# A hybrid decoder layer on one core: the output projection cut into two passes, one head group started later, and the low halves of a stretch of weights given to one engine

## The chip, the cores and the metric

The kernel runs on one core of one Trainium2 chip. The metric is the device time of one execution in microseconds, the median of several executions; lower is better. The engines are TensorE (PE in the rows; PEld its weight loads), VectorE (DVE), ScalarE (ACT), GpSimd (POOL), and SyncE (SP), which here only issues DMAs.

## What is computed

One layer on a sequence of T = 256 tokens of width D = 2048, in fp32:

```python
mod = silu(c) @ w_ada + b_ada         # shift, scale, gate for the mixer and for the FFN
h = rms_norm(x) * (1 + scale_m) + shift_m
p = h @ w_in                          # 14 blocks of 512 columns and 16 low-rank columns
o_gla = 4 heads of chunked gated linear attention (key 128, value 256)
o_hg  = 8 heads of chunked gated recurrence (key 128, value 128)
y = concat(rms_norm(o_gla) * silu(g_gla), rms_norm(o_hg) * silu(g_hg)) @ w_out
x = x + gate_m * y
h = rms_norm(x) * (1 + scale_f) + shift_f
a, u = split(h @ w_ffn_in)            # 2 x 5632 columns
x = x + gate_f * ((silu(a) * u) @ w_ffn_out)
return rms_norm(x)
```

## The kernel before

**Products in three matmuls.** Each fp32 factor is split in a high half (rounded to fp32r by a ScalarE copy, L206) and a low half (the rest, by a subtraction, L208). A product is low activation times high weight, high times high, and high times low (L249 to L251). Weights come in *halves* of 128x2x512 (512 KB, one DMA on SP each, L219), five ahead (`load_ahead`), and `next_half` splits them `SPLIT_AHEAD` = 3 halves ahead of their use. `low_on_pool(i)` says which engine subtracts the low half of split number i: GpSimd for seven of eight below 80, for three of four up to 210, VectorE for the rest. A half is worth 12 matmuls of 512 columns on TensorE: two token tiles, two channel tiles, three products.

**Stages.** (1) Load of x, its norm, and the first two channels of the modulation. (2) The input projection in six groups of channels (`K_GROUPS`); while one group is multiplied, `side.tick()` runs steps of the modulation for the next (`ada_channel`: VectorE multiplies and adds 128x512 pieces of `w_ada`, L126; `make_h` builds h). Splits 0 to 67 belong to groups 0 to 4, 68 to 87 to the last group, 88 to 111 to the late blocks g0, g1, s0, s1. (3) From the last group on, three *tasks* run beside the products, the GLA heads (`gla_group`) and two groups of four HGRN2 heads (`hg_group`): each call of `advance()` takes every task one step on. `scores` builds decay-weighted score matrices in seven levels; each is two ScalarE copies, two or three VectorE multiplications (L484, L486, L492), eight small matmuls (L469) and a predicated copy (L474). At its end stand two more predicated copies (L504), then `head_outputs` (L519, L521) and `gated`, which leaves the split activations y: acts 0 to 3 from GLA, acts 4 to 7 from HGRN2. (4) The output projection (splits 112 to 143), one bank of 512 columns after the other, over all 16 channel tiles in `OUT_ORDER` (HGRN2 first, then GLA). (5) Residual and second norm: `row_rms` (VectorE sum, a GpSimd power at L288), `row_diag` (ScalarE, L344), and matmuls with that diagonal (L350). (6) The FFN (splits from 144) and the final norm.

**Order.** The order of each engine's queue is fixed when the kernel is built, by a scheduler that plans with modelled durations and the order in which the program names the work; at run time each engine takes its queue in order. In stage 1 SP's and VectorE's queues are written out by hand. `issue_after(i)` puts an instruction behind i in its engine's queue. Work tiles are *slabs* from a pool of 33; the product banks in PSUM are two.

```python
OUT_ORDER = (8, 12, 0, 4)
...
y_act = [acts[i] for i in range(8)]
...
for b in range(4):
    pst = mm_apart(f"mm_out_{b}") if b == 3 else mm_bank(f"mm_out_{b}")[1]
```

Of the kernel before, what the change touches and what calls it, by code (L numbers as in the profile page):

```python
# [25 lines left out]
P = 128  # L26
# [19 lines left out]
EARLY_SPLIT = ("out_3_0", "out_3_4", "f1_0_1_0", "f2_3_9", "f2_3_10")  # L46
WARM = (24, 10)
ADA_HELD = "f1_0_1_0"
CONST_HELD = "in_f0_8"
POOL_END = 210  # L50

GLA_Q, GLA_K, GLA_V, GLA_G, GLA_LR = 0, 512, 1024, 2048, 3072
# [5 lines left out]
def hybrid_layer(ctx: ExitStack, tc: tile.TileContext, x, c, w_ada, b_ada, norm_mix_w, w_in,  # L58
# [129 lines left out]
    pending = []  # L188
    n_used = [0]

    def next_half():

        i = n_used[0]
        n_used[0] += 1
        while True:
            load_ahead()
            early = 4 if pending and pending[0][1][:-2] in EARLY_SPLIT else 0
            if not pending or n_split[0] >= i + 1 + SPLIT_AHEAD + early:
                break
            raw, name = pending.pop(0)  # L200
            if early:
                hi, lo = (slab(f"{n}_{name}", (P, 2, 512), F32R) for n in ("hi", "lo"))
            else:
                hi, lo = (split.tile([P, *raw.shape[1:]], F32R, tag=n, name=f"{n}_{name}")
                          for n in ("hi", "lo"))
            nc.scalar.activation(hi, raw, AF.Copy)  # L206
            eng = nc.gpsimd if low_on_pool(n_split[0]) else nc.vector
            eng.tensor_tensor(out=lo, in0=raw, in1=hi.bitcast(F32), op=ALU.subtract)  # L208
            ready[n_split[0]] = hi, lo
            n_split[0] += 1  # L210
        return ready.pop(i)
# [18 lines left out]
    def low_on_pool(i):  # L230
        return i < POOL_END and (i % 8 != 4 if i < 80 else i % 4 != 0)

# [5 lines left out]
    def products_of(items, act, first, last):  # L238

        items = [(ps, [(k, next_half()) for k in ks]) for ps, ks in items]  # L240
        for t in range(NT):
            for ps, halves in items:
                for c, o in ps[t]:
                    for i, (k, (hi, lo)) in enumerate(halves):
                        for j in range(2):
                            a = act[k // 2][:, j]
                            xh, xl = a[:, 0, t * P:(t + 1) * P], a[:, 1, t * P:(t + 1) * P]
                            end = last and i == len(halves) - 1 and j == 1
                            nc.tensor.matmul(o, xl, hi[:, j, c], start=first and i + j == 0, stop=False)  # L249
                            nc.tensor.matmul(o, xh, hi[:, j, c], start=False, stop=False)  # L250
                            nc.tensor.matmul(o, xh, lo[:, j, c], start=False, stop=end)  # L251

# [20 lines left out]
    def transpose_pair(src, j0, name):  # L273
# [6 lines left out]
        return pt  # L280

    def inv_rms(ss, n, cnt, name):

        m = sm.tile([P, n], F32, tag="ms", name=f"m_{name}")
        r = sm.tile([P, n], F32, tag="rr", name=f"r_{name}")
        nc.vector.tensor_scalar(out=m, in0=ss, scalar1=1.0 / cnt, scalar2=EPS, op0=ALU.mult,
                                op1=ALU.add)
        nc.gpsimd.tensor_tensor(out=r, in0=m, in1=neg_half[:, 0:n], op=ALU.pow)  # L288
        return r
# [27 lines left out]
    for name in late:  # L317
        for k0 in range(done_k[name], KT, 4):
            chunks.append((w_in_v, k0, 4, blocks[name], 512, f"in_{name}_{k0}"))
    OUT_ORDER = (8, 12, 0, 4)  # L320
    for b in range(4):
        for k0 in OUT_ORDER:
            chunks.append((w_out_v, k0, 4, b * 512, 512, f"out_{b}_{k0}"))
    nf = FFN // 512
# [5 lines left out]
    for half, (ja, jb) in enumerate(ffn_parts):  # L330
# [4 lines left out]
        for b in range(4):  # L335
            for j in range(ja, jb):
                chunks.append((w_f2_v, 4 * j, 4, b * 512, 512, f"f2_{b}_{j}"))

    def row_diag(r, name):

        n = r.shape[1]
        diag = slab(f"diag{name}", (P, n, P))
        for t in range(n):
            nc.scalar.activation(diag[:, t], ident, AF.Copy, scale=r[:, t:t + 1])  # L344
        return [diag[:, t] for t in range(n)]
# [6 lines left out]
    def warm(n, name):  # L352

        pw = bank(f"warm{name}", (P, P))
        for _ in range(n):
            nc.tensor.matmul(pw, ones_r, ones_r, start=True, stop=True)

# [14 lines left out]
    with tc.manual_schedule(engines={mybir.EngineType.SP, mybir.EngineType.DVE}):  # L372
        ada0 = ada_channel(0, 0, 2)
        for q in range(4):
            nc.sync.dma_start(out=xs[q], in_=xv[:, :, q * 512:(q + 1) * 512])
            next(ada0)
# [21 lines left out]
        next(ada0)  # L398
        load_ahead(2)
        next(ada0)  # L400
# [12 lines left out]
    def make_h(which, src, diags, dst):  # L413
        def make(ka, kb):
            for k in range(ka, kb, 2):
                pt = bank(f"pth{which}_{k}", (P, 2, T))
                for t in range(NT):
                    normed(pt[:, :, t * P:(t + 1) * P], src[k // 4][:, t], k % 4, diags[t])
                for j in range(2):
                    affine(pt[:, j], which, k + j)  # L420
                split_pair(pt, dst[k // 2])
        return make
# [134 lines left out]
    h_act = [act_slab(f"h{i}") for i in range(KT // 2)]  # L557

    pt0 = [bank(f"pth0_{j}", (P, 1, T)) for j in range(2)]
    for j in range(2):  # L560
# [99 lines left out]

    def gla_group():
        F = yield from low_rank_decay()
        yield from until("k")
# [46 lines left out]
    for name in late:  # L710
        ps, pst = mm_bank(f"mm_in_{name}")
        for k0 in range(done_k[name], KT, 4):
# [8 lines left out]
            advance()  # L721
            side.tick()
    while tasks:
        advance()


    y_act = [acts[i] for i in range(8)]
    ssy = sm.tile([P, NT, 5], F32, name="ssy", bufs=1)
    x1 = []
    for b in range(4):  # L730
        pst = mm_apart(f"mm_out_{b}") if b == 3 else mm_bank(f"mm_out_{b}")[1]
        xq = slab(f"xr{b}")
        nc.scalar.dma_start(out=xq, in_=xv[:, :, b * 512:(b + 1) * 512])
        groups = [[k0, k0 + 2] for k0 in OUT_ORDER]
        if b == 3:
            groups[-2:] = [groups[-2] + groups[-1]]
        for g in groups:
            products(pst, y_act, g, g is groups[0], g is groups[-1])
            side.tick()
        for t in range(NT):  # L740
            for i, (n, o) in enumerate(pst[t]):
                nc.vector.tensor_tensor(out=o, in0=o, in1=gate_m[b][:, n], op=ALU.mult)
                nc.vector.tensor_tensor(out=xq[:, t, n], in0=o, in1=xq[:, t, n], op=ALU.add)
                junk = sm.tile([P, 512], BF16, tag="junk", name=f"junky_{b}_{t}_{i}", bufs=1)
                nc.scalar.activation(junk[:, n], xq[:, t, n], AF.Square,
                                     accum_out=ssy[:, t, b + i:b + i + 1])
        x1.append(xq)
    side.finish()
    ry = [row_rms(ssy[:, t, 0:4 + t], f"y{t}") for t in range(NT)]
# [24 lines left out]
    for q in range(4):  # L774
# [5 lines left out]
        for j in range(FFN_GROUPED):  # L780
            pss = [mm_bank(f"mm_f1_{j}_{w}_{q}") for w in range(2)]
            if q + j == 0:
                products_of([(pst, (0, 2)) for _, pst in pss], h2, True, True)
            for w, (ps, pst) in enumerate(pss):
# [112 lines left out]
```

## Time and profile before

| | |
|---|---|
| median of 3 runs | 1295.06 us (1292.39 to 1296.37) |
| the profiled execution's own time | 1293.13 us |
| its span, first to last instruction | 1291.3 us |
| busy: PE, PEld, DVE, ACT, POOL | 1234.4, 1028.7, 880.0, 599.2, 434.3 us |
| mean granted TensorE clock | 0.993 |
| read from HBM | 320.49 MB |

Busy time is a sum over stages with different limits. A matmul's end is modelled, so one of 512 columns counts as busy for 0.39 us although the next follows sooner. Idle time of an engine is put down to the instruction that released it.

### The profile page before, as it was taken

The numbers are of one execution on the slowest core, as the hardware profiler recorded it, in microseconds if no ns is written. First come the engines' busy times: TensorE is split into PE (matmuls) and PEld (weight loads), VectorE is DVE, ScalarE is ACT, GpSimd is POOL, SyncE is SP. The second block draws the span as 40 slices with busy tenths as digits, with TensorE's granted clock in tenths as the row PEclk, the third lists the DMA queues.
The fourth block names the chain that finished last, engine by engine and source line by source line (L and its number), as shares of the span: only waits on it lengthen the run. The fifth ranks groups of instructions, "written<-read, shape, count | busy, mean of one in ns | idle before, by whom it ended". The sixth has DMA issues, their size and how long they took to land.

```text
span 1291.3 us, 16066 instructions
## 1 busy us (share of the span) xinstructions
PE 1234.4 (96%) x5832; PEld 1028.7 (80%) x5832; DVE 880.0 (68%) x1025; ACT 599.2 (46%) x745; POOL 434.3 (34%) x198
## 2 busy tenths in 40 slices
PE   4999999998898999899999999999999999999996
PEld 3888888877777788788888788888888888888876
DVE  5489976569999575556685998796555455445653
ACT  5644344495543545455344345534334444443442
POOL 4577767543454567556666100000000000000010
PEclk9999999999999999999999999999999999999998
DMA  9999999845468698699998896696666556655661
GB/s 342 318 337 340 368 311 343 267 120 157 137 194 290 212 355 293 232 321 342 346 326 309 270 317 219 225 370 193 197 195 193 184 184 190 196 189 187 193 194 69
DMA packets 178536, 323.65 MB, mean 251 GB/s; under 512 B 12689, under 2 KB 29685, under 8 KB 178457
## 3 DMA queue, kind: packets, MB, share of 16 engines
q1 hardware_dynamic: 176888, 319.42, 72.9%
q10 hardware_dynamic: 1376, 3.15, 0.7%
q8 instruction: 46, 0.75, 0.2%
q14 instruction: 34, 0.27, 0.1%
q0 software_dynamic: 192, 0.06, 0.0%
HBM read 320.49 MB, written 2.10 MB: 250 GB/s over the span
## 4 chain that ended last, share of the span: by engine, by line
PE 56%; issue 1%; DVE 1%; ACT 0%; DMA 0%; ACTq 0%; POOLq 0%; POOL 0%
PE mm_f L249 18%; PE mm_f L251 18%; PE mm_f L250 18%; PE pthid L278 1%; PE pth L350 0%; DMA raw_f_a<-in_w_ffn_out_dram 0%; PE pada L146 0%; DVE lo_f_b L208 0%; ACT hi_f_b L206 0%; DVE xr L834 0%; PE pgate L179 0%; DVE mm_f L833 0%; ACT hi_f_a L206 0%; ACT junkf L837 0%; ACT ob L852 0%
## 5 line engine op out<-in xcount | busy, mean ns | idle before, releaser
L206 ACT ACTIVATE hi_f_a<-raw_f_a 128x1024 fp32r<-128x1024 f32 x132 | 140.1, 1061 | 332.5 <-PE mm_f L250 309.4
L208 DVE TENSOR_TENSOR lo_f_a<-raw_f_a,hi_f_a 128x1024 fp32r<-128x1024 f32 x116 | 147.2, 1269 | 202.7 <-ACT hi_f_a L206 201.8
L126 DVE SCALAR_TENSOR_TENSOR accada<-wada,c_act,accada 128x512 f32<-128x512 f32 x224 | 168.6, 753 | 24.4 <-DMA wada<-in_w_ada_dram 19.7
L206 ACT ACTIVATE hi_f_b<-raw_f_b 128x1024 fp32r<-128x1024 f32 x132 | 140.1, 1061 | 52.9 <-PE mm_f L250 44.5
L840 POOL TENSOR_TENSOR xr<-xr,fw 128x512 f32<-128x512 f32 x6 | 9.3, 1553 | 457.6 <-ACT junkf L837 457.6
L249 PE MATMUL mm_f<-hi_f_a,h 128*128 128x512 f32 x352 | 138.1, 392 | 1.0 <-ACT hi_f_b L206 1.0
L251 PE MATMUL mm_f<-lo_f_b,h 128*128 128x512 f32 x352 | 137.7, 391 | 0.0
L251 PE MATMUL mm_f<-lo_f_a,h 128*128 128x512 f32 x352 | 137.6, 391 | 0.0
L249 PE MATMUL mm_f<-hi_f_b,h 128*128 128x512 f32 x352 | 137.3, 390 | 0.0
L250 PE MATMUL mm_f<-hi_f_a,h 128*128 128x512 f32 x352 | 137.2, 390 | 0.0
L250 PE MATMUL mm_f<-hi_f_b,h 128*128 128x512 f32 x352 | 137.0, 389 | 0.0
L208 DVE TENSOR_TENSOR lo_f_b<-raw_f_b,hi_f_b 128x1024 fp32r<-128x1024 f32 x99 | 122.8, 1241 | 16.6 <-ACT hi_f_b L206 9.3
L208 POOL TENSOR_TENSOR lo_f_b<-raw_f_b,hi_f_b 128x1024 fp32r<-128x1024 f32 x33 | 80.7, 2445 | 39.8 <-ACT hi_f_b L206 32.4
L126 DVE SCALAR_TENSOR_TENSOR accadag<-wadag,c_act,accadag 128x512 f32<-128x512 f32 x112 | 84.2, 752 | 5.5 <-DMA wadag<-in_w_ada_dram 3.5
L249 PEld LDWEIGHTS mm_f<-hi_f_a,h 128*128 128x128 f32 x352 | 66.1, 188 | 14.6 <-ACT hi_f_b L206 1.4
L250 PEld LDWEIGHTS mm_f<-hi_f_b,h 128*128 128x128 f32 x352 | 66.1, 188 | 13.8
L251 PEld LDWEIGHTS mm_f<-lo_f_b,h 128*128 128x128 f32 x352 | 66.1, 188 | 13.6
L251 PEld LDWEIGHTS mm_f<-lo_f_a,h 128*128 128x128 f32 x352 | 66.1, 188 | 13.6
L250 PEld LDWEIGHTS mm_f<-hi_f_a,h 128*128 128x128 f32 x352 | 66.1, 188 | 13.4
L249 PEld LDWEIGHTS mm_f<-hi_f_b,h 128*128 128x128 f32 x352 | 66.1, 188 | 13.2
L249 PE MATMUL mm_f<-hi_f_a,hid 128*128 128x512 f32 (+1 forms) x186 | 70.4, 378 | 1.6 <-DVE xr L834 1.6
L251 PE MATMUL mm_f<-lo_f_b,hid 128*128 128x512 f32 (+1 forms) x186 | 70.2, 378 | 1.0 <-DVE lo_f_b L208 1.0
(386 smaller groups left out, 2848.5 us busy)
## 6 DMA issues: line engine op xcount, KB each, us to landing
wada<-in_w_ada_dram SPq DMA_DIRECT2D x96, 512.0 KB, 6.1
raw_f_a<-in_w_ffn_in_dram SPq DMA_DIRECT2D x88, 512.0 KB, 4.6
raw_f_b<-in_w_ffn_in_dram SPq DMA_DIRECT2D x88, 512.0 KB, 4.4
wadag<-in_w_ada_dram SPq DMA_DIRECT2D x64, 512.0 KB, 6.5
raw_f_a<-in_w_ffn_out_dram SPq DMA_DIRECT2D x44, 512.0 KB, 4.8
raw_f_b<-in_w_ffn_out_dram SPq DMA_DIRECT2D x44, 512.0 KB, 3.9
wada<-in_w_ada_dram SPq DMA_DIRECT2D x64, 256.0 KB, 6.1
raw_out_a<-in_w_out_dram SPq DMA_DIRECT2D x16, 512.0 KB, 6.3
```

The lines of the kernel that those rows point to most:

```text
L126: nc.vector.scalar_tensor_tensor(out=dst, in0=raw[:, j], scalar=ck, in1=acc if k else bias, op0=ALU.mult, op1=ALU.add)
L206: nc.scalar.activation(hi, raw, AF.Copy)
L208: eng.tensor_tensor(out=lo, in0=raw, in1=hi.bitcast(F32), op=ALU.subtract)
L249: nc.tensor.matmul(o, xl, hi[:, j, c], start=first and i + j == 0, stop=False)
L250: nc.tensor.matmul(o, xh, hi[:, j, c], start=False, stop=False)
L251: nc.tensor.matmul(o, xh, lo[:, j, c], start=False, stop=end)
L278: nc.tensor.transpose(pt[:, j, t * P:(t + 1) * P], src[:, t, (j0 + j) * P:(j0 + j + 1) * P], ident)
L840: nc.gpsimd.tensor_tensor(out=xt, in0=xt, in1=fw[b // 2][:, b % 2], op=ALU.mult)
```

## The change

The output projection runs in two passes. The first multiplies only the HGRN2 channels (k 8 to 15) for all four banks and copies each sum to a slab `part_o`; then come the GLA channels (k 0 to 7), and `part_o` is added at the evacuation (for the last bank it is gated and added to x beforehand). The load order of `w_out` follows. `gla_group` waits 12 calls of `advance()` before it begins. Splits 76 to 115 take their low halves on VectorE. The instructions of the first FFN product, its splits among them, are queued behind the second norm's power, diagonal and last split; splits keep their order; the norm matmuls of `make_h` are queued behind the last product issued. At the start, x is loaded through ScalarE's queue, one half of weights instead of two goes ahead of the last pieces of modulation, and the warming matmuls are 8 and 5 of 512 columns instead of 24 and 10 of 128.

```diff
-WARM = (24, 10)
+WARM = (8, 5)
+GLA_DELAY = 12
+MIXER_LOW = (76, 116)
...
-            nc.scalar.activation(hi, raw, AF.Copy)
             eng = nc.gpsimd if low_on_pool(n_split[0]) else nc.vector
-            eng.tensor_tensor(out=lo, in0=raw, in1=hi.bitcast(F32), op=ALU.subtract)
+            for ins in (nc.scalar.activation(hi, raw, AF.Copy),
+                        eng.tensor_tensor(out=lo, in0=raw, in1=hi.bitcast(F32), op=ALU.subtract)):
+                tc.stamp_issue_order_token(ins.ins, "split")
...
     def low_on_pool(i):
-        return i < POOL_END and (i % 8 != 4 if i < 80 else i % 4 != 0)
+        if i < MIXER_LOW[0]:
+            return i % 8 != 4
+        return MIXER_LOW[1] <= i < POOL_END and i % 4 != 0
...
-    OUT_ORDER = (8, 12, 0, 4)
-    for b in range(4):
-        for k0 in OUT_ORDER:
-            chunks.append((w_out_v, k0, 4, b * 512, 512, f"out_{b}_{k0}"))
+    out_phases = ((8, 12), (0, 4))
+    for b, k0 in [(b, k0) for ks in out_phases for b in range(4) for k0 in ks]:
+        chunks.append((w_out_v, k0, 4, b * 512, 512, f"out_{b}_{k0}"))
...
     def warm(n, name):
-        pw = bank(f"warm{name}", (P, P))
+        pw = bank(f"warm{name}")
         for _ in range(n):
-            nc.tensor.matmul(pw, ones_r, ones_r, start=True, stop=True)
+            nc.tensor.matmul(pw, ones_r, x_r, start=True, stop=True)
...
-            nc.sync.dma_start(out=xs[q], in_=xv[:, :, q * 512:(q + 1) * 512])
+            nc.scalar.dma_start(out=xs[q], in_=xv[:, :, q * 512:(q + 1) * 512])
...
-        load_ahead(2)
+        load_ahead(1)
...
-                for t in range(NT):
-                    normed(pt[:, :, t * P:(t + 1) * P], src[k // 4][:, t], k % 4, diags[t])
+                with tc.issue_after(last_mm[0].ins):
+                    for t in range(NT):
+                        normed(pt[:, :, t * P:(t + 1) * P], src[k // 4][:, t], k % 4, diags[t])
...
     def gla_group():
+        for _ in range(GLA_DELAY):
+            yield
...
+    while any(i not in acts for i in range(4, 8)):
+        advance()
+    for b in range(4):
+        ps, pst = mm_bank(f"mm_out_{b}")
+        for k0 in out_phases[0]:
+            products(pst, acts, (k0, k0 + 2), k0 == out_phases[0][0], k0 == out_phases[0][-1])
+            advance()
+            side.tick()
+        part_o.append(slab(f"po_{b}"))
+        nc.scalar.activation(part_o[b], ps, AF.Copy)
     while tasks:
         advance()
+    side.finish()
     for b in range(4):
-        pst = mm_apart(f"mm_out_{b}") if b == 3 else mm_bank(f"mm_out_{b}")[1]
+        last = b == 3
+        pst = mm_apart(f"mm_out2_{b}") if last else mm_bank(f"mm_out2_{b}")[1]
...
+        groups = [[k0, k0 + 2] for k0 in out_phases[1]]
+        for g in [groups[0] + groups[1]] if last else groups:
+            products(pst, acts, g, g[0] == 0, g[-1] == 6)
+        if last:
+            for t in range(NT):
+                nc.vector.tensor_tensor(out=part_o[b][:, t], in0=part_o[b][:, t], in1=gate_m[b], op=ALU.mult)
+            nc.vector.tensor_tensor(out=xq, in0=xq, in1=part_o[b], op=ALU.add)
         for t in range(NT):
             for i, (n, o) in enumerate(pst[t]):
+                if not last:
+                    nc.vector.tensor_tensor(out=o, in0=o, in1=part_o[b][:, t, n], op=ALU.add)
...
             if q + j == 0:
-                products_of([(pst, (0, 2)) for _, pst in pss], h2, True, True)
+                with tc.issue_after(made_r[0].ins), tc.issue_after(made_d[0].ins), \
+                        tc.issue_after(h2_made.ins):
+                    products_of([(pst, (0, 2)) for _, pst in pss], h2, True, True)
```

## Rows read from the trace of the kernel before

**Rows 1.** Page, part 1: busy time, share and instructions of each engine.
```profile
PE 1234.4 (96%) x5832; PEld 1028.7 (80%) x5832; DVE 880.0 (68%) x1025; ACT 599.2 (46%) x745; POOL 434.3 (34%) x198
```
**Rows 2.** Windows: stretch, length, busy (instructions) by engine, granted clock, DMA share, GB/s.
```profile
241.00:447.00 206.00, 187.25 (x968) 154.91 (x967) 171.51 (x216) 115.44 (x197) 91.34 (x40) 0.98 0.59 193
...
290.00:424.00 134.00, 117.89 (x625) 99.71 (x626) 130.74 (x171) 65.83 (x115) 58.36 (x25) 0.96 0.61 199
...
447.00:528.00 81.00, 80.15 (x398) 66.84 (x396) 49.14 (x60) 39.84 (x51) 59.41 (x24) 1.00 0.87 318
```
**Rows 3.** Waits of PE, 241 to 455 us: total, times, longest.
```profile
PE po_hg L519 <- DVE sc_hg L504: 6.7, 3, 4.1
```
**Rows 4.** Groups of DVE instructions, 241 to 447 us: busy, mean ns, idle before.
```profile
L126 DVE SCALAR_TENSOR_TENSOR accadag<-wadag,c_act,accadag 128x512 f32<-128x512 f32 x28 | 21.1, 753 | 0.7
L486 DVE TENSOR_TENSOR p_q<-p_q,t_hg 128x512 f32<-128x512 f32 x12 | 14.6, 1213 | 0.7 <-ACT t_hg L482 0.7
...
L484 DVE TENSOR_TENSOR p_k<-p_k,t_gla 128x512 f32<-128x512 f32 x6 | 7.9, 1312 | 0.0
L504 DVE COPY_PREDICATED sc_hg<-masks,m_hg 128x512 f32<-128x512 uint8 x4 | 7.7, 1973 | 0.0
```
**Rows 5.** Lines L486 and L504, all instructions: duration ns min/median/max, first and last start.
```profile
L486 DVE TENSOR_TENSOR p_q<-p_q,t_hg x12: 673/679/2857, 286.1 to 365.5; 128x512 f32<-128x512 f32 x12
...
L504 DVE COPY_PREDICATED sc_hg<-masks,m_hg x4: 712/2160/2859, 360.1 to 399.5; 128x512 f32<-128x512 uint8 x4
```
**Rows 6.** Timeline of POOL and DVE, near 322 us: start, duration, instruction.
```profile
322.35 2.40 POOL L208 TENSOR_TENSOR lo_in_g_a<-raw_in_g_a,hi_in_g_a 128x1024 fp32r<-128x1024 f32 x1 [5.28 <-ACT hi_in_g_a L206]
...
322.56 2.73 DVE L486 TENSOR_TENSOR p_q<-p_q,t_hg 128x512 f32<-128x512 f32 x1
```
**Rows 7.** Timeline of PE, 394 to 406 us.
```profile
399.76 2.19 PE L519 MATMUL po_hg<-p_i,sc_hg 128*128 128x128 f32 x10 [4.14 <-DVE sc_hg L504]
```
**Rows 8.** Line L208 on DVE, one of its groups.
```profile
L208 DVE TENSOR_TENSOR lo_in_g_a<-raw_in_g_a,hi_in_g_a x2: 1210/1212/1214, 317.6 to 333.6; 128x1024 fp32r<-128x1024 f32 x2
```
**Rows 9.** Timeline of all engines, 518 to 548 us.
```profile
527.95 0.16 DVE L286 TENSOR_SCALAR m_y<-ss_y 128x1 f32<-128x1 f32 x1
528.23 2.35 POOL L208 TENSOR_TENSOR lo_f_b<-raw_f_b,hi_f_b 128x1024 fp32r<-128x1024 f32 x1 [1.56 <-PE mm_out L251]
...
530.53 0.55 POOL L288 TENSOR_TENSOR r_y<-m_y,neg_half 128x1 f32<-128x1 f32 x1
...
531.57 1.61 PE L350 MATMUL pth<-diagy,xr 128*128 128x128 f32 x12 [3.36 <-ACT diagy L344]
```
**Rows 10.** Windows of the start.
```profile
2.00:8.00 6.00, 0.26 (x1) 0.18 (x1) 0.00 (x0) 2.93 (x7) 2.52 (x6) 1.00 0.80 244
8.00:40.00 32.00, 20.79 (x92) 19.04 (x93) 22.30 (x41) 14.48 (x28) 10.09 (x5) 1.00 1.07 394
```
**Rows 11.** Timeline of the start and of 28 to 36 us.
```profile
15.00 0.37 SPq L219 DMA_DIRECT2D raw_in_f_b<-in_w_in_dram  x1
...
33.29 0.63 PE L249 MATMUL mm_in_f<-hi_in_f_b,h 128*128 128x512 f32 x1
33.72 0.63 PE L250 MATMUL mm_in_f<-hi_in_f_b,h 128*128 128x512 f32 x1
...
37.68 0.39 PE L249 MATMUL mm_in_f<-hi_in_f_b,h 128*128 128x512 f32 x1
...
37.91 0.39 PE L250 MATMUL mm_in_f<-hi_in_f_b,h 128*128 128x512 f32 x1
```
**Rows 12.** Tiles ptc_q, y_g, ptc_k, y_s: duration ns min/median/max, first and last start.
```profile
L278 PE MATMUL ptc_q<-ident,p_q x24: 270/272/329, 257.4 to 291.3; 128*128 128x128 f32 x24
...
L267 DVE TENSOR_TENSOR y_g<-pty_g,y_g x4: 684/684/685, 385.0 to 421.5; 128x512 fp32r<-128x512 f32 x4
...
L278 PE MATMUL ptc_k<-ident,p_k x8: 270/272/330, 276.8 to 280.0; 128*128 128x128 f32 x8
...
L267 DVE TENSOR_TENSOR y_s<-pty_s,y_s x4: 686/689/693, 443.5 to 456.9; 128x512 fp32r<-128x512 f32 x4
```

More of the change, by code (lines that the diff above doesn't have):

```diff
@@ L189, in hybrid_layer @@
     n_used = [0]
+    last_mm = [None]
     def next_half():
@@ L250, in products_of @@
                             nc.tensor.matmul(o, xh, hi[:, j, c], start=False, stop=False)
-                            nc.tensor.matmul(o, xh, lo[:, j, c], start=False, stop=end)
+                            last_mm[0] = nc.tensor.matmul(o, xh, lo[:, j, c], start=False, stop=end)
     def mm_bank(name):
@@ L280, in transpose_pair @@
         return pt
+    made_r = [None]
     def inv_rms(ss, n, cnt, name):
@@ L287, in inv_rms @@
                                 op1=ALU.add)
-        nc.gpsimd.tensor_tensor(out=r, in0=m, in1=neg_half[:, 0:n], op=ALU.pow)
+        made_r[0] = nc.gpsimd.tensor_tensor(out=r, in0=m, in1=neg_half[:, 0:n], op=ALU.pow)
         return r
@@ L337, in hybrid_layer @@
                 chunks.append((w_f2_v, 4 * j, 4, b * 512, 512, f"f2_{b}_{j}"))
+    made_d = [None]
     def row_diag(r, name):
@@ L343, in row_diag @@
         for t in range(n):
-            nc.scalar.activation(diag[:, t], ident, AF.Copy, scale=r[:, t:t + 1])
+            made_d[0] = nc.scalar.activation(diag[:, t], ident, AF.Copy, scale=r[:, t:t + 1])
         return [diag[:, t] for t in range(n)]
@@ L557, in hybrid_layer @@
     h_act = [act_slab(f"h{i}") for i in range(KT // 2)]
+    x_r = slab("x_r", (P, 512), F32R)
+    nc.scalar.activation(x_r, xs[0][:, 0], AF.Copy)
     pt0 = [bank(f"pth0_{j}", (P, 1, T)) for j in range(2)]
@@ L722, in hybrid_layer @@
             side.tick()
+    while any(i not in acts for i in range(4, 8)):
+        advance()
+    ssy = sm.tile([P, NT, 5], F32, name="ssy", bufs=1)
+    x1 = []
+    part_o = []
+    for b in range(4):
[6 more added lines that the diff above has]
+        nc.scalar.activation(part_o[b], ps, AF.Copy)
     while tasks:
         advance()
-    y_act = [acts[i] for i in range(8)]
-    ssy = sm.tile([P, NT, 5], F32, name="ssy", bufs=1)
-    x1 = []
+    side.finish()
     for b in range(4):
-        pst = mm_apart(f"mm_out_{b}") if b == 3 else mm_bank(f"mm_out_{b}")[1]
+        last = b == 3
+        pst = mm_apart(f"mm_out2_{b}") if last else mm_bank(f"mm_out2_{b}")[1]
         xq = slab(f"xr{b}")
         nc.scalar.dma_start(out=xq, in_=xv[:, :, b * 512:(b + 1) * 512])
[L734 to L739, printed above, removed]
+        groups = [[k0, k0 + 2] for k0 in out_phases[1]]
[5 more added lines that the diff above has]
+            nc.vector.tensor_tensor(out=xq, in0=xq, in1=part_o[b], op=ALU.add)
         for t in range(NT):
             for i, (n, o) in enumerate(pst[t]):
+                if not last:
+                    nc.vector.tensor_tensor(out=o, in0=o, in1=part_o[b][:, t, n], op=ALU.add)
                 nc.vector.tensor_tensor(out=o, in0=o, in1=gate_m[b][:, n], op=ALU.mult)
@@ L747, in hybrid_layer @@
         x1.append(xq)
-    side.finish()
     ry = [row_rms(ssy[:, t, 0:4 + t], f"y{t}") for t in range(NT)]
```

## The prediction, made before the result was known

> **What bounds the kernel now.** I read the page's sums first: TensorE is busy for 1234 of 1291 us [rows 1], so a change can only win what TensorE waits for or does slowly. The windows in stretches of 20 us then show where that is. From 40 to 240 us and from 540 to 1240 us it hardly waits. What is lost lies in four places: the first 20 us, the mixer from 241 to 447 us, the second norm near 530 us, and the tail, which the change leaves alone.
>
> In the mixer TensorE is busy for 187.3 of 206 us, so 18.8 us are idle [rows 2]. In its dense part, 290 to 424 us, the granted clock is 0.96 on average; the other stretches stand at or near 1.00. It drops three times to the lower of its two levels (1.2 instead of 2.4 GHz), each time in or after a wait of some 3 to 4 us; at 0.96 this costs 134 x 0.04 = 5.4 us. A matmul counts as busy for 0.39 us but the next starts 0.23 us later [rows 11], so each wait hides some 0.16 us; about 16 waits make 2.6. The mixer's loss is 18.8 + 5.4 + 2.6 = 27 us.
>
> The releasers name VectorE: the largest wait is for `sc_hg`, 6.7 us in three pieces [rows 3], and in the dense part VectorE is busy for 130.7 of 134 us, while GpSimd works for 58 [rows 2]. Why it is full shows in its groups. The same 128x512 multiplication takes 0.68 us at the median and 2.86 at the longest; the predicated copy 0.71 and 2.86 [rows 5]. The long ones lie under a GpSimd subtraction: GpSimd starts at 322.35 for 2.40 us, VectorE's 0.68 us multiplication at 322.56 takes 2.73 [rows 6]. It waits the other out. The longest PE wait, 4.14 us before 399.76 [rows 7], stands behind two such operations. The additions from PSUM (L126, 0.75 us) show no such spread [rows 4].
>
> **The change part by part.**
>
> *Low halves on VectorE.* Of splits 76 to 115, 30 move from GpSimd to VectorE, at 1.21 us each [rows 8]: 36.3 us more there. What comes back is the time lost under GpSimd. Of the groups in [rows 4], L486 has 14.6 - 12 x 0.68 = 6.4 us of it, `p_k` 7.9 - 6 x 0.68 = 3.8, L504 7.7 - 4 x 0.71 = 4.9; five groups of the same kind add about 16. That is some 31 us for some 34 GpSimd subtractions in this stretch (91 us busy there [rows 2], at 2.4 us, less the powers), 0.9 each, so 30 fewer give back 27. The ledger of VectorE from 241 to 447 us goes from 171.5 to 171.5 + 36.3 - 27 = 181 us: the move is nearly paid for, it does not relieve VectorE.
>
> The Trainium skill's Perfetto Trace Analysis, section Optimizing Scalar/DVE Operations, speaks against the move: it says that work of a saturated VectorE may go to GpSimd, and adds that it might not help, since the two share a port. By its first half 30 x 1.21 us would come on top; by its second half the refund above is right. No row shows the changed split, so the first half is a rival below.
>
> *Two passes and later GLA heads.* The cover is the gain. Before, four halves of output projection (one bank's HGRN2 channels) stood ahead of the first need of GLA's y; after, sixteen. Twelve more halves at 12 x 0.227 = 2.72 us are 33 us of products. TensorE's own work up to that need is 206 - 27 + 33 = 212 us, VectorE's 181: 85%. But the dense part stays dense. There VectorE has 130.7, with 22 low halves at +1.21 and -0.9 each, +7, and less what GLA moves out: its seven to eight later calls, each one block of two halves, put about half of its roughly 20 us of operations past the end, -10. That makes 128, and TensorE's own need is 117.9 - 7 = 111. The 17 us too much are stalls, unless the 28 gate additions of 0.75 us [rows 4], 21 us, step aside; they now have until the second pass evacuates. Bounds: 0 stall if all step aside, 17 if none do. I take the middle, 8.5. So the mixer gains 27 - 8.5 = 18.5 us (10 to 27).
>
> The new operations cost little: four ScalarE copies of about 1 us (that engine is busy for 46% [rows 1]), six additions of 0.68 [rows 5] on VectorE in the second pass, and three operations for the last bank made before its sums are ready. All lie beside 43.6 us of products, a stretch in which VectorE was busy for 49 of 81 us [rows 2]; if that cover is gone, they cost 2 x 0.68 for a bank.
>
> *Splits behind the norm.* At 527.95 VectorE gives the sum for the power, but GpSimd has just begun a low half at 528.23, for 2.35 us; the power runs at 530.53, and TensorE starts the norm's matmuls at 531.57 after 3.36 us [rows 9]. With that split queued behind, the power runs about 2.35 us earlier, and the first token tile with it: gain 2.4. What is queued behind: `next_half` has split the four halves of the first FFN product earlier (`EARLY_SPLIT` holds the second block), so only the next three wait, with 48 x 0.227 = 10.9 us of products in front of them. Their loads come as much later; the DMA share stood at 0.87 before it [rows 2]. Bounds: 0 if the second token tile ends last, 3.4 if the whole wait goes.
>
> *The start.* From 8 to 40 us the DMAs run at 394 GB/s, so a half that stands ahead delays what is behind it by 0.524 MB / 394 GB/s = 1.3 us. `raw_in_f_b` stood ahead of the last modulation pieces [rows 11], which feed the first product; now it doesn't. From 2 to 8 us only 244 GB/s moved [rows 10], 6 x 150 GB/s = 0.9 MB or 2.3 us short; x issued from a second queue wins part of it. I take 0.7, between nothing and 2.3. The Trainium skill's DMA: Bandwidth & Descriptors, section Issuing engines are not separate DMA queues, says that this saves only the issuer's time, by which the term is at most the four issues, 4 x 0.37 = 1.5 us by the row of one [rows 11]. Six early products run 0.43 us apart, the lower clock, against 0.23 later [rows 11]; if the wide warming matmuls raise the clock sooner, that is 6 x 0.2 = 1.2; fewer of them may as well let it stay low, -1.5. I take 0.5. Start: 2.5 us (-1.5 to 4.8). Moving the norm matmuls of `make_h` and fixing the order of splits I cost at nothing: products fill TensorE in those stages, and without that cover one such matmul is 0.11 us.
>
> **The sum.** 18.5 + 2.4 + 2.5 = 23.4. The profiled execution took 1293.1 us (its span 1291.3), so 1269.7. The median of the runs is 1.9 above that execution: 1271.6, rounded 1271.
>
> **The rivals.**
>
> *VectorE stays the bound.* Then the lost time only changes its place: products wait for low halves instead of score matmuls for VectorE. For: VectorE at 130.7 of 134 us, and the low halves join that queue. From 241 to 528 us it had 220.7 us of work (171.5 + 49.1); after, 220.7 + 36.3 - 27 + 7 = 237. At the share it reached in the mixer, 171.5/206 = 0.83, this takes 285 of the 287 us. Only start and norm gain: 1295 - 2 - 4.9 = 1288. Against: GLA's part moves to where it was 61% busy.
>
> *All mixer waits go.* The cover takes everything, as it would if the plan, which knows no waiting under GpSimd, now holds: 1295 - 27 - 5 to 8 = 1260, or lower by what I undercount.
>
> *GLA is late* (the slower side). It runs from 276.8 (`ptc_k`) to 457 us (`y_s`), 180 us [rows 12]. Eight calls later, at some 6.6 us of TensorE each, it starts at 330, and TensorE reaches the second pass at about 241 + 212 = 453. So 123 us are covered. The first HGRN2 group took 257.4 to 385, 128 us, while three shared VectorE [rows 12]. At 128 TensorE waits 5 us; from 123 + 31 = 154 us on, the wait eats the whole gain; at 180 it is 57, and the time 1295 - 31 + 57 = 1321. Against: it runs alone once HGRN2 is through.
>
> *No refund* (also slower). If VectorE's long operations had another cause than GpSimd, 237 + 27 = 264 us at 0.83 need 318, 31 more than 287: 1295 + 31 - 5 = 1321. The row at 322.56 speaks against it [rows 6].
>
> **Numbers.** Forecast 0.56, VectorE bound 0.17, all waits gone 0.14, GLA late 0.08 (some of it within the range), no refund 0.03, other 0.02. The range 1257 to 1288 takes in the first three but for the edges. 0.3% is 3.9 us, about what a measurement tells from no change. Faster: the first three less some of the second, 0.84; same 0.07; slower 0.09.
>
> **What would show it.** Right: in the dense stretch no 0.68 us operation of VectorE above 1.3 us, GpSimd nearly empty there, VectorE still over 90%, PE idle and clock drops at a third; all `po_gla` and `pty_s` within the first pass; the power within 0.5 us of its sum; a first product before 30.5 us. Wrong: PE waits for low halves from `L208` on VectorE, or for `y_s` at the head of the second pass; a power still behind a split.

## The result, and the profile after

The changed kernel is slower: 1309.26 us at the median of four runs (1308.19 to 1309.46), against 1293.72 for the kernel before beside it. The ratio is 1.0124, with a 95% interval from 1.0099 to 1.0149. The forecast was 1271 (its sum gives 1271.6), and even the upper end of its range was 1288. The profiled execution took 1309.23 us, its span 1307.3.

The page's sums, which answer to [rows 1], show the same work in a longer span: TensorE is busy for 1233.7 us (1234.4 before), GpSimd for 77 us less.

```profile
PE 1233.7 (94%) x5787; PEld 1027.3 (79%) x5787; DVE 894.9 (68%) x1064; ACT 607.5 (46%) x751; POOL 357.2 (27%) x168
```

So the loss is in waits and in clock. Windows of the changed kernel, columns as in [rows 2]:

```profile
241.00:380.00 139.00, 139.00 (x754) 118.22 (x753) 120.20 (x166) 87.55 (x134) 7.31 (x4) 1.00 0.71 219
380.00:470.00 90.00, 64.01 (x303) 50.53 (x302) 79.82 (x115) 39.97 (x78) 19.38 (x10) 0.83 0.57 187
470.00:526.00 56.00, 56.00 (x247) 46.01 (x246) 25.41 (x21) 28.91 (x34) 40.27 (x16) 1.00 0.68 225
526.00:545.00 19.00, 9.84 (x66) 9.15 (x65) 10.29 (x21) 7.37 (x19) 6.98 (x5) 0.91 0.60 224
```

The dense part came out better than hoped. From 241 to 380 us TensorE is never idle and the granted clock is 1.00; the last product of the mixer ends at 390.8 us, before it was 430.6, in part because GLA's operations now come later. All of this is lost again afterwards. From 380 to 470 us TensorE idles for 26 us at a mean clock of 0.83, and from 526 to 545 us for 9 more. What it waits for in the first of these stretches, by the view of waits (total, times, longest), where [rows 3] showed 6.7 us for `sc_hg`:

```profile
PE pty_g L284 <- DVE p_g L549: 9.7, 1, 9.7
PE po_gla L529 <- DVE p_v L541: 6.6, 1, 6.6
PE pty_s L284 <- DVE p_s L549: 3.5, 1, 3.5
PE pty_s L284 <- DVE y_s L273: 1.7, 1, 1.7
PE po_gla L529 <- DVE sc_gla L514: 1.7, 1, 1.7
```

and from 520 to 546 us:

```profile
PE mm_out L255 <- DVE xr L772: 4.9, 1, 4.9
PE pth L359 <- DVE h L273: 4.3, 1, 4.3
```

A last one stands far from all edits, at 833 us: 3.7 us for `hi_f_b` on ScalarE. The first product of the FFN starts at 544.6 us where it was 535.1 before, 9.5 later; from there to the end it takes 6.5 us longer. These two make the 16 us between the spans.

Three rows answer to [rows 5]. What was held up to 2.86 us under GpSimd now runs at its own speed in the dense part. GLA's predicated copies, which now come at 437 us, beside low halves of split 116 and later, are held again:

```profile
L496 DVE TENSOR_TENSOR p_q<-p_q,t_hg x12: 683/690/699, 268.9 to 326.1; 128x512 f32<-128x512 f32 x12
...
L514 DVE COPY_PREDICATED sc_hg<-masks,m_hg x4: 733/738/743, 316.8 to 381.4; 128x512 f32<-128x512 uint8 x4
L514 DVE COPY_PREDICATED sc_gla<-masks,m_gla x2: 732/1801/2870, 437.0 to 437.6; 128x512 f32<-128x512 uint8 x2
```

And two to [rows 12], first transposition and last `y` of GLA: it runs from 363.3 to 464.4 us, 101 us in all.

```profile
L284 PE MATMUL ptc_k<-ident,p_k x8: 272/272/328, 363.3 to 369.4; 128*128 128x128 f32 x8
...
L273 DVE TENSOR_TENSOR y_s<-pty_s,y_s x4: 681/682/684, 455.7 to 463.7; 128x512 fp32r<-128x512 f32 x4
```

### The profile page after: what moved, and what is told of

Same layout as the page of the kernel before. It is cut to its first block, busy times and chain, and to the rows that moved or that the text cites. A ratio compares the mean times of both kernels' runs of the same rounds, so it can differ in the third digit from the quotient of the medians.

```text
span 1307.3 us, 15998 instructions
## 1 busy us (share of the span) xinstructions
PE 1233.7 (94%) x5787; PEld 1027.3 (79%) x5787; DVE 894.9 (68%) x1064; ACT 607.5 (46%) x751; POOL 357.2 (27%) x168
## 4 chain that ended last, share of the span: by engine, by line
PE 85%; DVE 6%; DMA 3%; issue 3%; POOL 1%; ACT 1%; ACTq 0%; POOLq 0%; DVEq 0%; SPq 0%
PE mm_f L257 18%; PE mm_f L255 18%; PE mm_f L256 18%; DVE accadag L128 2%; PE mm_in_q L255 2%; PE mm_in_q L257 2%; PE mm_in_q L256 2%; PE mm_out L255 1%; PE mm_out L256 1%; PE mm_out L257 1%; PE mm_in_i L257 1%; PE mm_in_i L255 1%; PE mm_in_g L255 1%; PE mm_in_v L255 1%; PE mm_in_i L256 1%
## 5 line engine op out<-in xcount | busy, mean ns | idle before, releaser
L211 DVE TENSOR_TENSOR lo_f_a<-raw_f_a,hi_f_a 128x1024 fp32r<-128x1024 f32 x116 | 149.9, 1292 | 208.0 <-ACT hi_f_a L210 207.6
L128 DVE SCALAR_TENSOR_TENSOR accadag<-wadag,c_act,accadag 128x512 f32<-128x512 f32 x112 | 84.1, 751 | 1.7 <-DMA wadag<-in_w_ada_dram 0.2
L256 PEld LDWEIGHTS mm_f<-hi_f_a,h 128*128 128x128 f32 x352 | 66.4, 189 | 13.5
L257 PEld LDWEIGHTS mm_f<-lo_f_b,h 128*128 128x128 f32 x352 | 66.1, 188 | 13.5
L255 PE MATMUL mm_f<-hi_f_b,hid 128*128 128x512 f32 (+1 forms) x186 | 70.6, 380 | 3.7 <-ACT hi_f_b L210 3.7
```

What stands on the lines that cost most here:

```text
L128: nc.vector.scalar_tensor_tensor(out=dst, in0=raw[:, j], scalar=ck, in1=acc if k else bias, op0=ALU.mult, op1=ALU.add)
L257: last_mm[0] = nc.tensor.matmul(o, xh, lo[:, j, c], start=False, stop=end)
```

## The experiments

The theory at the start (A): TensorE does its products in an order that is written out in advance. GLA's last products stand in it behind the first 96 of the 192 products of the first pass and ahead of the other 96, which need nothing of GLA. VectorE, fuller by the low halves and by GLA's later work, reaches them late. Its rivals: the 30 low halves alone are the price (B), the later GLA alone (C), the two passes (D). Runs under one heading share a chip and its runs of the kernel before, whose median goes from 1292.5 to 1295.5 us between headings; a difference of runs under two headings is that uncertain. The ratios are to the kernel before on the same chip.

### First runs: which part costs

The changed kernel with the old rule for low halves (in it, GpSimd's old share of splits 76 to 115):

```
-MIXER_LOW = (76, 116)
+MIXER_LOW = (80, 80)
```

> The changed kernel with the low halves of splits 76 to 115 shared with GpSimd by the old rule; all else stays. Theory A (TensorE's queue is written out in advance, and GLA's last products stand in it ahead of products of the first pass that need nothing of GLA; VectorE, made fuller by the 30 low halves and by GLA's later work, reaches them late): the stalls under GpSimd come back in the dense part, but VectorE has 36 us less, so the ends of HGRN2 and GLA come earlier; 1300 to 1308. Theory B (the 30 low halves on VectorE alone are the price): at or under the kernel before, 1285 to 1294. Theory C (the later GLA) or D (the two passes) alone: no gain, 1305 to 1312.

1316.01 us, ratio 1.0173 [1.0145, 1.0202]: some 7 us slower than the changed kernel. B is wrong, and so are the numbers of A, C and D for this run: the last product of the mixer ends 26 us later than in the changed kernel, at 416.8 us. The stalls under GpSimd cost more than VectorE's 36 us less bring.

The changed kernel with `GLA_DELAY = 0`:

> The changed kernel with GLA's group started without the twelve calls of delay; the low halves stay on VectorE and the two passes stay. Theory A: the ends of GLA come before pass 1, but then HGRN2 and GLA share VectorE as before, and the mixer waits there; about 1295 to 1304. Theory C (the delay alone is what costs): 1280 to 1290. B or D: unchanged, 1305 to 1312.

1293.95 us, 1.0007 [0.9989, 1.0026], a little under A's numbers and above C's. The delay costs 15 us.

Both together:

> The changed kernel with neither the delay nor the moved low halves: what is left is the two passes, the splits behind the norm and the other start. Theory D (the two passes with their additions cost the time): 1300 or more. Theory A, B or C: the mixer is the one of before, with a little cover more, and start and norm give their 2 to 5 us: 1284 to 1293.

1303.55 us, 1.0080 [1.0048, 1.0111]. So the rest of the change is not free either: it loses 11 us against the kernel before. That is D's number, but it doesn't say which part of the rest it is.

The kernel before, with only the low halves moved:

```
     def low_on_pool(i):
+        if 76 <= i < 116:
+            return False
```

> The kernel before, with the low halves of splits 76 to 115 all on VectorE and nothing else changed. Theory B (no refund, or not enough of it): 1305 to 1325. Theory A, with the refund that the prediction worked out (36.3 us paid, 27 back): 1288 to 1300, and no 0.68 us operation of VectorE above 1.3 us in the dense part.

1284.58 us, 0.9931 [0.9908, 0.9954]: alone, the move gains 8 us. Window and predicated copies of this run, to be set beside [rows 2] and [rows 5]:

```profile
241.00:447.00 206.00, 193.34 (x1012) 162.42 (x1011) 176.25 (x257) 121.36 (x203) 22.93 (x13) 0.97 0.64 203
```
```profile
L506 DVE COPY_PREDICATED sc_hg<-masks,m_hg x4: 720/730/736, 357.8 to 395.1; 128x512 f32<-128x512 uint8 x4
```

VectorE does 41 instructions more, 30 of them the low halves, in 4.7 us more. The refund is real.

### Second runs: the rest of the change, one part at a time

The base of all four is the kernel before with the low halves on VectorE (1284.58 us, on the first chip); each run adds one part of the diff ahead of the prediction, word for word.

The two passes alone:

> The kernel before with the low halves of the mixer on VectorE (1284.6 us) and the two passes alone. If the wait of 5.5 us ahead of the last bank's second pass (the evacuation of two banks with three operations for each token tile, under GpSimd's low halves) comes from the passes, as their trace says: 1284.6 + 5 to 8 = 1290 to 1293. If it comes from the other queue of splits: 1284 to 1287, with no wait over 2 us there.

1284.60 us, 0.9909 [0.9877, 0.9941]. No cost that can be measured. TensorE waits 2.2 us ahead of the last bank:

```profile
PE mm_out L251 <- DVE xr L757: 2.2, 1, 2.2
```

In the run without the delay, which has all other parts as well, it is 5.1:

```profile
PE mm_out L255 <- DVE xr L772: 5.1, 1, 5.1
```

The norm's reordering alone, its matmuls and its splits:

> The same base and the order of the second norm alone: the first FFN products' splits behind the power, the diagonals and the first pair, and the norm's matmuls behind the products ahead of them. If the prediction's step holds: 2.4 us less, 1282. If the wait only moves to the second token tile's pair (4.5 us of it stood there in the changed kernel): 1284 to 1287.

1289.30 us, 0.9958 [0.9942, 0.9973]. Slower than the base, and neither expectation has the number. At 813 us TensorE waits 3.7 us for `hi_f_b`, as the changed kernel does at 833.

The fixed order of splits alone (`stamp_issue_order_token`):

> The same base and nothing but the fixed order of the splits, which the prediction costed at nothing. If it is what makes the product of the FFN's second half wait 4 us for its high half on ScalarE: 1288 to 1291, with that wait in the trace. If it is free: 1284 to 1286.

1283.36 us, 0.9903 [0.9877, 0.9929]. Free by itself; no wait at 810 us.

The start alone:

> The same base and the other start alone (x issued by ScalarE's queue, one chunk loaded ahead instead of two, 13 wide warming matmuls). By the prediction 2.5 us less: 1282. By the trace of the changed kernel, whose first product comes 1.2 us later but at the full clock at once: 1284 to 1285.

1282.18 us, 0.9893 [0.9866, 0.9921]. About the 2.5 us of the prediction, against a base on another chip; 1.2 to 2.4 us under the two runs with passes or fixed order on its own.

### Third runs: the queue, and the two halves of the norm's reordering

The changed kernel, with GLA's last products spread among the first pass:

```
     def gla_group():
 ...
         SC, X = yield from scores(Q, K, F, "gla")
         yield from until("v0", "v1")
+        for _ in range(4):
+            yield
         ons = head_outputs(SC, X, [parts["v0"], parts["v1"]], GLA_DV, nw_gla, "gla")
```

> The changed kernel with four more idle calls between GLA's scores and its head outputs, so that its last products stand in TensorE's queue between products of the first pass and no longer ahead of the last 96 of them. Theory A (the queue's order is what the later GLA costs): of the 17 us lost from 440 to 466 us, clock included, 10 to 14 come back: 1295 to 1299. Rival (GLA is late, whatever stands in front): the wait moves to the head of the second pass with its size: 1305 to 1312.

1294.08 us, 0.9995 [0.9983, 1.0006]. Four idle calls give back 15.2 us, and not one operation less is done. Waits of this run from 380 to 475 us, beside those of the changed kernel above:

```profile
PE pty_g L284 <- DVE p_g L549: 9.7, 1, 9.7
PE pty_s L284 <- DVE p_s L549: 1.6, 1, 1.6
PE po_gla L529 <- DVE p_v L541: 1.3, 1, 1.3
...
PE mm_out L255 <- ACT po L753: 0.8, 1, 0.8
```

The wait for `p_v` goes from 6.6 to 1.3 us, that for `p_s` from 3.5 to 1.6, and the 20.5 us at the lower clock from 446 us on are gone. Now 120 products of the first pass stand ahead of GLA's last ones, and the other 72 between and behind them, the next at once:

```profile
444.35 1.03 PE L529 MATMUL po_gla<-p_v,sc_gla 128*128 128x256 f32 x4
445.03 0.58 PE L255 MATMUL mm_out<-hi_out_a,y_g 128*128 128x512 f32 x1
```

GLA itself is no earlier: its last `y` is ready at 471.1 us, 464.4 in the changed kernel. At the head of the second pass TensorE waits 0.8 us (for `po`, on ScalarE). The rival is out.

Only the norm's matmuls held behind the products ahead of them, on the base of the second runs:

```
                 pt = bank(f"pth{which}_{k}", (P, 2, T))
-                for t in range(NT):
-                    normed(pt[:, :, t * P:(t + 1) * P], src[k // 4][:, t], k % 4, diags[t])
+                with tc.issue_after(last_mm[0].ins):
+                    for t in range(NT):
+                        normed(pt[:, :, t * P:(t + 1) * P], src[k // 4][:, t], k % 4, diags[t])
```

> The kernel before with the low halves on VectorE (1284.6 us) and only the norms' matmuls held behind the products that stand ahead of them. If this is the half of the norm's reordering that costs, through the order in which the planner then puts ScalarE's work near 810 us (the hidden's pieces ahead of the high halves): 1288 to 1291, with the wait of 4 us at 810. If it is free: 1282 to 1286.

1288.83 us, 0.9952 [0.9935, 0.9969]. The wait is there, at 810 to 814 us:

```profile
PE mm_f L252 <- ACT hi_f_b L207: 3.7, 1, 3.7
```

Only the splits held behind the norm:

> The same base and only the splits of the first FFN products held behind the power, the diagonals and the first pair. If the prediction's step holds: 1282, with no wait at 810. If the wait goes to the second token tile's pair: 1284 to 1287.

1283.92 us, 0.9909 [0.9892, 0.9925]. On the same chip the two differ by 4.9 us, and the place is on ScalarE's timeline. First the run with the matmuls held:

```profile
809.45 0.60 ACT L269 ACTIVATE hid<-pthid 128x512 fp32r<-128x512 f32 x1 [6.61 <-PE pthid L281]
...
811.54 1.06 ACT L173 ACTIVATE hi_gate<-adag 128x1024 fp32r<-128x1024 f32 x1 [1.00 <-DVE adag L126]
812.50 1.04 ACT L207 ACTIVATE hi_f_b<-raw_f_b 128x1024 fp32r<-128x1024 f32 x1
```

then the one with the splits held:

```profile
805.64 1.06 ACT L206 ACTIVATE hi_f_b<-raw_f_b 128x1024 fp32r<-128x1024 f32 x1 [3.01 <-PE mm_f L252]
...
809.50 0.59 ACT L268 ACTIVATE hid<-pthid 128x512 fp32r<-128x512 f32 x1
```

In the slower one two pieces of the hidden layer and a high half of the gate stand ahead of `hi_f_b`. The pieces wait 6.61 us for transpositions, which stand on TensorE behind products; `hi_f_b`, for which TensorE waits next, starts only at 812.50. In the other `hi_f_b` goes first. It is the planner that wrote these two orders, from edits 290 us earlier. Why the held matmuls lead it to the worse one isn't shown.

The changed kernel without the delay and without the norm's reordering:

> The same base with the two passes, the fixed order of splits and the other start, that is the changed kernel without the later GLA and without the norm's reordering. If the parts add up as measured alone (0, -1, -2.4): 1280 to 1283. If the passes and the fixed order hurt each other at the last bank (5.5 us there in the kernel without the delay): 1286 to 1289.

1284.87 us, 0.9921 [0.9905, 0.9936], between the two expectations. Passes, start and fixed order do not quite add up; the wait at the last bank is 5.1 us again.

### Fourth runs: the wait near 400 us, and the best combination

The base of the second runs with the other start and the held splits:

> The kernel before with the low halves on VectorE, the other start and the splits behind the norm; no two passes, no later GLA, no fixed order of splits, the norm's matmuls where they were. If the parts add up as measured alone (1284.6, less 2.4, less 0.7 to 2): 1280 to 1282, the fastest so far.

**1281.01 us, 0.9892 [0.9863, 0.9922]. It beats both kernels**: 13.6 us under the kernel before beside it.

The same with the steps of modulation and gates (`side.tick`) left out from the fifth level of HGRN2's second group until its heads are gated, and caught up after that:

```
             self.i += 1
+            if hold[0]:
+                return
             want = self.steps * self.i // self.units
```

> The same, with the steps of modulation and gates held from the fifth level of HGRN2's second group until its heads are through. If the gate additions are what TensorE waits for near 400 us (8.4 us): the wait falls to 4 to 5 and the time by 3 to 6 us. If it is the serial chain (squares, power, scaling, gating, transposes) behind the last scores: the wait stays at 7 or more, and the gates come later at the evacuations, 0 to 10 us slower.

1284.83 us, 0.9920 [0.9892, 0.9948]. TensorE's wait for `p_g` falls from 8.1 to 5.2 us, and the run is 3.8 us slower all the same.

The changed kernel with GLA's ends spread, the norm's matmuls where they were and the order of splits free:

> The changed kernel with GLA's ends spread among the first pass (1294.1 us), the norm's matmuls where they were and the splits' order free again. If those two are the 5 to 6 us at 810 and the 2.7 us at the last bank: 1285 to 1288. If the waits belong to the later GLA: 1291 to 1295.

1289.15 us, 0.9952 [0.9935, 0.9969], a little above the first expectation: 4.9 us less than with them, on another chip. The wait at 810 us is gone, that at the last bank is 2.3. But beside it on the same chip the kernel without the two passes and the later GLA is still 8.1 us faster (1281.01).

And this one with the gate steps held:

> The same with the gate steps held as in c1_hold4. If the gate additions hold up the end of HGRN2 (ten of them, 7.7 us, in the 12.9 us before its gating): the wait of 10 us falls to 4 to 6, and the time by 4 to 6 us, unless the gates' 32 additions then meet GLA's operations in the first pass and give it back there.

1291.76 us, 0.9979 [0.9962, 0.9996]. Its waits from 380 to 475 us, and then from 475 to 530:

```profile
PE po_gla L529 <- DVE p_v L541: 4.9, 1, 4.9
PE pty_g L283 <- DVE p_g L549: 4.5, 1, 4.5
```
```profile
PE mm_out L254 <- DVE xr L780: 7.6, 2, 6.6
```

The wait for `p_g` falls from 9.6 to 4.5 us, and the evacuations give it back: 7.6 us there instead of 2.3.

## Why the prediction was wrong, point by point

**Low halves: right in kind, and worth more than was said.** The rival without a refund is out. The ledger said 181 us for VectorE from 241 to 447 us; alone the move left it at 176.25, and 183.0 in the changed kernel. That bears out what [rows 6] showed: of the multiplications and predicated copies that stood up to 2.86 us before, none lasts over 0.75 us in the run with that part alone. The Trainium skill's SBUF — State Buffer, section Who interferes with whom, says that a VectorE instruction with two inputs in SBUF contends with a GpSimd instruction that reads SBUF, and one with at most one such input, outside the two-port modes, does not. The traces agree: the products of two tiles ran up to 2.86 us [rows 5], and the kernel before has one operation in both forms, with its second input in PSUM (`accadag`) and, at the head of a sum, in SBUF (`adag`):

```profile
L126 DVE SCALAR_TENSOR_TENSOR accadag<-wadag,c_act,accadag x28: 740/756/756, 381.1 to 419.6; 128x512 f32<-128x512 f32 x28
...
L126 DVE SCALAR_TENSOR_TENSOR accadag<-wadag,c_act,adag x2: 761/1534/2306, 378.8 to 403.7; 128x512 f32<-128x512 f32 x2
```

The prediction said of this move that it does not relieve VectorE, and put its 18.5 us on the cover. The move alone earns 8; the cover earned nothing.

**Later GLA heads: this step failed.** The prediction counted "twelve more halves" as cover, and let TensorE wait for GLA only at its first need, the head of the second pass. Its slower rival had the right mechanism's name and the wrong place. By it GLA would start at 330 us, with 123 us until the second pass. GLA started at 363.3 and took 101, so by that rival 11 us would have been lost, at the second pass. The waits came in the middle of the first, 13.5 us from 440 to 461. What decides is that the products of the cover have to stand ahead in TensorE's queue. Half of them stood behind GLA's ends. Undoing the delay gives 15.3 us, spreading the ends alone 15.2 (15 and 17 by the ratios). The Trainium skill's PSUM — Partial Sum Buffer, section Engine vs sequencer instructions, says that matmuls start and complete in program order. The changed kernel's timeline agrees: from 443.1 to 450.0 us no matmul starts. The next four halves of the first pass, 48 products, were split by 442.7 us, and the first of these products runs at 464.6:

```profile
442.46 1.03 PE L529 MATMUL po_gla<-p_v,sc_gla 128*128 128x256 f32 x4
450.04 1.22 PE L529 MATMUL po_gla<-p_v,sc_gla 128*128 128x256 f32 x2 [6.55 <-DVE p_v L541]
...
464.60 1.17 PE L255 MATMUL mm_out<-hi_out_a,y_g 128*128 128x512 f32 x1
```

Most of the prediction's signs of being right came true: no held operation and no idle TensorE in the dense part, all `po_gla` and `pty_s` within the first pass. None asked how many products stood in front of them.

The prediction also moved GLA to where GpSimd takes low halves again (from split 116 on), and gave that no price. Four operations of GLA that take 0.69 to 0.74 us by themselves last 1.98, 2.84, 2.82 and 2.87 there, at 415, 420, 425 and 437 us, each beside a subtraction on GpSimd: 7.7 us of GLA's 101. They are held as long in the run with the ends spread, so they are not what that run gave back; a kernel that keeps those low halves on VectorE too was not run.

**The gate additions did not step aside.** The prediction took 8.5 us of stalls, "0 if all step aside, 17 if none do". VectorE's timeline ahead of the longest wait of the changed kernel, 390.8 to 400.5 us:

```profile
387.29 3.93 DVE L128 SCALAR_TENSOR_TENSOR accadag<-wadag,c_act,accadag 128x512 f32<-128x512 f32 x5
391.12 1.22 DVE L211 TENSOR_TENSOR lo_out_a<-raw_out_a,hi_out_a 128x1024 fp32r<-128x1024 f32 x1
392.26 0.75 DVE L128 SCALAR_TENSOR_TENSOR accadag<-wadag,c_act,accadag 128x512 f32<-128x512 f32 x1
392.92 1.22 DVE L211 TENSOR_TENSOR lo_out_b<-raw_out_b,hi_out_b 128x1024 fp32r<-128x1024 f32 x1
...
394.13 2.33 DVE L128 SCALAR_TENSOR_TENSOR accadag<-wadag,c_act,accadag 128x512 f32<-128x512 f32 x3
396.37 2.15 DVE L541 SCALAR_TENSOR_TENSOR p_i<-po_hg,r_hg,nw_hg 128x128 f32<-128x128 f32 x8
398.44 0.75 DVE L128 SCALAR_TENSOR_TENSOR accadag<-wadag,c_act,accadag 128x512 f32<-128x512 f32 x1
399.09 1.22 DVE L549 TENSOR_TENSOR p_g<-p_g,p_i 128x1024 f32<-128x1024 f32 x1
```

Ten additions stand ahead of `p_g`. Held back, they free 5.1 of its 9.6 us; the other half is the chain itself, with the low halves in it. But the gates are due at the evacuations, so they can't wait: both runs that held them became 2.6 to 3.8 us slower. The wait is not the later GLA's: the run with the low halves alone already has 8.1 us of it, where the kernel before waited 4.1 for `sc_hg`. Nothing covers the end of HGRN2 in any of them.

**Two passes: cost at nothing, true only alone.** With the free order of splits, and gates that are not held, the evacuation of two banks costs a wait of 2.2 to 2.3 us and no time that can be measured. With the fixed order it is 4.9 to 5.4 us in six kernels, whatever else they have. VectorE's timeline of the changed kernel shows the place:

```profile
523.99 3.29 DVE L766 TENSOR_TENSOR xr<-xr,po 128x1024 f32<-128x1024 f32 x1
527.20 0.69 DVE L770 TENSOR_TENSOR mm_out<-mm_out,po 128x512 f32<-128x512 f32 x1
```

The operation for the last bank that was to be "made before its sums are ready" stands in VectorE's queue ahead of the third bank's evacuation. So that starts at 527.2 us, 0.5 after TensorE ran out of products (526.7); in the run with the passes alone it starts at 508.3, 1.7 ahead of that (510.0). Why the fixed order shifts it isn't shown.

**Splits behind the norm: not shown to do what was said.** In the changed kernel the power comes 0.23 us after its sum, as forecast, where [rows 9] had 2.58. But the second token tile is then last. All engines of the changed kernel:

```profile
533.91 0.15 DVE L294 TENSOR_SCALAR m_y<-ss_y 128x1 f32<-128x1 f32 x1
534.14 0.55 POOL L296 TENSOR_TENSOR r_y<-m_y,neg_half 128x1 f32<-128x1 f32 x1 [4.66 <-DVE m_y L294]
...
542.35 0.55 POOL L296 TENSOR_TENSOR r_y<-m_y,neg_half 128x1 f32<-128x1 f32 x1 [5.25 <-DVE m_y L294]
...
544.12 0.71 PE L359 MATMUL pth<-diagy,xr 128*128 128x128 f32 x4 [4.26 <-DVE h L273]
```

The prediction gave this as its lower bound, 0. From the last product of the output projection to the first of the FFN it is 6.9 us before and 5.6 after. By itself the part measured 0.7 us under its base, on another chip: nothing that can be told from no change. There the power still stands behind a low half, which the prediction had named as a sign of being wrong:

```profile
512.99 2.41 POOL L208 TENSOR_TENSOR lo_f_b<-raw_f_b,hi_f_b 128x1024 fp32r<-128x1024 f32 x1 [2.84 <-ACT hi_f_b L206]
513.75 0.15 DVE L290 TENSOR_SCALAR m_y<-ss_y 128x1 f32<-128x1 f32 x1
515.34 0.56 POOL L292 TENSOR_TENSOR r_y<-m_y,neg_half 128x1 f32<-128x1 f32 x1
```

And the run without the norm's reordering, but with the fixed order, has its power 0.23 us after the sum too. So the 0.23 can't be put to the held splits.

**The norm's matmuls: cost at nothing, measured 4 to 5 us.** They cost 4.9 us against the held splits on one chip, 4.2 against their base on another. "Products fill TensorE in those stages" was true and beside the point. The order in which the planner then wrote ScalarE's queue has a wait of 3.7 us in it, 290 us further on, and the lower clock behind it (3.4 us of it at 814 us). In the changed kernel without the delay the norm's reordering as a whole costs 9.1 us, on two chips (1293.95 with it, 1284.87 without), more than its parts show alone. The term that was left out is what a changed plan does elsewhere.

**The start: the number came out, how isn't shown.** 2.4 us were measured for 2.5 forecast. But in the run with the start alone the first product starts at 31.5 us, where the base has 31.6 and the prediction's sign asked for 30.5; in the changed kernel it is 33.1. The term for the clock is in the traces: the first twelve products take 2.7 to 2.8 us in five runs with the other start, 4.6 to 5.2 in five without it (all with the norm's matmuls where they were). By the 201st product that lead is gone: it starts at 81.4 to 84.1 us in the five, and at 81.8 to 83.5 without. The intervals of the runs with and without overlap, too. So the term's agreement is luck, or at least no proof of its parts.

The 38 us between forecast and result, from run to run: 15.2 for the queue (1309.26 to 1294.08), 4.9 for the norm's matmuls and the fixed order of splits (to 1289.15), and 8.1 for the two passes and the later GLA heads that are then still in the kernel (to 1281.01, on the same chip). The passes alone cost nothing that can be measured, so these 8.1 are put to the later GLA; its trace has 4.1 us of wait for `p_v` and 2.3 at the last bank that the other hasn't. The last 10 lie between 1281.01 and 1271: of the 23.4 us forecast, low halves, start and held splits earn 13.6, and the cover nothing.

## What to carry to other kernels

Work that is to cover a late producer must stand ahead of its consumer in the engine's queue, not only be independent of it: count the instructions in front of the first that waits, not those before the last need. Where a planner writes the queues, an edit that costs nothing where it is made can reorder another engine hundreds of microseconds away, so each part of a change is timed alone and the orders of all engines are compared. And an engine relieved in its dense part shows next what follows that part: here HGRN2's end, which nothing covered.

## What the runs showed of the hardware

In the changed kernel the granted clock stays low for longer than the waits last. It stands at the lower of its two levels, 1.2 GHz, from 394.8 to 405.0 us, in and behind a wait of 9.7 us, and from 446.0 to 466.5 us, through three waits of 6.6, 1.7 and 3.5 us. Columns as in [rows 2]:

```profile
446.00:466.50 20.50, 10.95 (x30) 7.56 (x31) 17.96 (x30) 5.57 (x11) 2.01 (x2) 0.50 0.51 186
```

The three drops of the kernel before were 3.4 us each. With the same waits broken up among products, the second stretch does not occur. A wait of 7 us cost TensorE twice: once idle, and again in what it did next: the matmul pairs of `po_gla` came 0.43 us apart ahead of that wait (441.2 us) and 0.86 behind it (451.1 us).
